# One program order for TensorE through the mixer, and the output projection in two parts instead of three

## The chip, the cores and the metric

The kernel runs on one core of a Trainium2 chip. The metric is the device time of one execution in microseconds: the median of three runs before the change is 1916.03 us (1914.43 to 1919.23). Line numbers are those of the kernel before, except where a line is said to be of the kernel after.

## What is computed

One layer of a hybrid decoder, with 256 positions of width 2048 in float32: a feed-forward half step, a mixer of differential attention (8 heads) beside RWKV-7 (16 heads of size 64), and a second feed-forward half step, each with a residual and a LayerNorm. The parts that matter here, cut from the reference:

```python
#  x <- LN1(alpha*x + 0.5*SwiGLU_1(x))
#  x <- LN2(alpha*x + W_out [DiffAttn(x) || RWKV7(x)])
#  x <- LN3(alpha*x + 0.5*SwiGLU_2(x))
...
# RWKV-7, per position t and head, after the token shift pr + mu * (prev - pr):
def step(state, xs):
    r_t, w_t, k_t, v_t, kk_t, a_t = xs
    sa = einsum('bhvk,bhk->bhv', state, -kk_t)
    state = state * w_t + sa * (kk_t * a_t) + v_t * k_t
    return state, einsum('bhvk,bhk->bhv', state, r_t)
...
# attention: two score maps for each head, p = softmax(s1) - lam * softmax(s2), then p @ v
```

One input projection, of 2048 rows, makes the columns of both mixers: q, k and v of attention, r, k and v of RWKV and 288 low-rank columns. The output projection, 2048 by 2048, joins them.

## The kernel before

**The weight stream.** Each large product is a stream of weight steps. A step loads two slices of 128 rows by up to 512 columns; ScalarE casts them to `wh` (L143) and VectorE takes the rest `wl` (L146). TensorE then makes six matmuls of 128x512 for one of the two tiles of 128 positions, hi by hi, hi by lo and lo by hi (L153 to L155), and six for the other tile of a step that lies two steps back in the mixer (`LAG`). A step in full flow is thus twelve large matmuls, called big matmuls below. When an accumulator is complete, its callback runs (`done(tt, acc)`).

**Blocks of the mixer.** The input projection is done block by block: the low-rank columns, then k, r, v of RWKV group 0 (8 heads), k and q of attention group 0, k and r of RWKV group 1, v of attention 0, v of RWKV 1, and k, q, v of attention 1 (L1098 to L1107). A callback copies its accumulator to SBUF (`tm`, L580), transposes it in four pieces (L584), and copies the result to `praw` (L608, L609 for the low-rank columns, L665 for r, k, v). After the second tile, `shift` makes the mix with the position before in one cycle for each of four pieces: ScalarE scales to `df` (L590), VectorE adds (L596). There is one `df` buffer.

**Background generators.** All other work of the mixer is written as Python generators that are advanced between weight steps by `run_bg`. `rwkv_group` makes the decay products and sigmoids (L731, L735), the scan (L739), the norm of k (scaling L745, square L746, product with a block of ones L753), the exponentials and products L760 to L779, the scores (`L789`, from AR and BK, masked to Q in L792), an inverse of 32 by 32 triangles on VectorE (`U`, `Y`, L828 to L839, here called the solve), transposes of BK (L811), and the recurrence over four chunks (L885 to L933): a product (L890), one with the inverse (L898), the state's addition and scaling (L906 to L916), the outputs (L923, L929). Then come the group norm (L945, L955) and the gate (L976, L979). `rwkv_values` transposes v (L701) and makes the bonus term (L713). `attn_heads` does the scores (L1027), softmax, transposes (L1050), product with v (L1059 to L1061), and norm.

**What sets the order.** In the input projection each generator has a credit (`BG` 1.6 for RWKV, `AT` 0.5 for attention) that a step adds to and each piece of work draws on; the instructions are then placed on each engine by the scheduler of the compiler's tile layer, which may put a group ahead of or behind where the program has it. In the first two of three parts of the output projection, `even` lets each generator do one piece for each step, and TensorE's order is fixed by hand there (`manual_schedule`, L1164). VectorE, ScalarE, GpSimd and the queues are always placed by the scheduler.

**The output projection.** Its 2048 rows are four quarters: attention 0, attention 1, RWKV 0, RWKV 1. `parts` (L1125) takes them as quarters 0 and 2, then 1, then 3. For each part and each of four column blocks, `o_done` (L1134) adds the accumulator to `y`; in the last part it does the LayerNorm statistics and the tail. A part of two quarters has eight slices of 128 rows, four pairs, so 24 matmuls for an accumulator and tile; a part of one has half of that. `ready(q)` (L1114) drains the generators of a quarter and splits its result into `xh` and `xl` (L89, L90).

Of the kernel before, what the change touches and what calls it, by code (L numbers as in the profile page):

```python
# [16 lines left out]
P = 128  # L17
# [18 lines left out]
BG = 1.6  # L36
AT = 0.5


def build(tc, A, out):  # L40
# [58 lines left out]
    class Stream:  # L99
        def __init__(self):  # L100
            self.pend = []
            self.tail = []
            self.roles = None
            self.behind = []
            self.acc = {}
            self.bg = []
            self.credit = {}
            self.hooks = {}
            self.step = 0
            self.slot = 0  # L110
            self.even = False
            self.hold = {}

# [157 lines left out]
        def flush(self, lag=0):  # L271
# [9 lines left out]
            while self.pend:  # L281
                self.mm(self.pend.pop(0), 1)

        def spawn(self, gen, rate):
            self.bg.append(gen)
            self.credit[gen] = [0.0, rate]

        def run_bg(self):
            if self.even:
                for g in list(self.bg):  # L290
                    if self.hold.get(g):
                        self.hold[g] -= 1
                        continue
                    while g in self.bg:
                        try:
                            if next(g) != 0:
                                break
                        except StopIteration:
                            self.bg.remove(g)
                return  # L300
            for g in list(self.bg):
                c = self.credit[g]
                c[0] = min(c[0], 0.0) + c[1]
                while c[0] > 0 and g in self.bg:
                    try:
                        cost = next(g)
                    except StopIteration:
                        self.bg.remove(g)
                        break
                    if cost is None:  # L310
                        break
                    c[0] -= cost
# [246 lines left out]
    def mix(mp, pq, C):  # L559
# [17 lines left out]
        def chan_major(acc, tt, widths, dst):  # L577
# [3 lines left out]
            tr = bank("tr", (P, 4, P))  # L581
            o = 0
            for i, w in enumerate(widths):
                T.transpose(tr[:w, i, :], tm[:, o:o + w], ident)  # L584
                o += w
            dst(tr)
# [12 lines left out]
        def lora_done(tt, acc):  # L599
            if tt == 0:  # L600
                pr = hp.tile([P, 4, S + 1], F32, tag="J1", name=nm("praw"))
                V.memset(pr[:, :, 0:1], 0.0)
                lora["raw"] = pr
            pr = lora["raw"]

            def dst(tr):
                c = slice(1 + tt * P, 1 + (tt + 1) * P)
# [3 lines left out]
            chan_major(acc, tt, [P, P, 32], dst)  # L611
            if tt == 1:
# [12 lines left out]
                lora.update(tw=tw, g1=g1, g2=g2)  # L625

# [20 lines left out]
        def rwkv_start(g, prev=None):  # L647
# [5 lines left out]
            stream.spawn(st["gen"], BG)  # L653
            return st

        def rwkv_cols(g, st, parts):
            gr = st["group"]

            def done(tt, acc, i):
                if tt == 0:  # L660
                    pr = hp.tile([P, 4, S + 1], F32, tag="J1" if g == 0 and i == 2 else "H3", name=nm("praw"))
                    V.memset(pr[:, :, 0:1], 0.0)
                    st["raw"] = pr
                pr = st["raw"]
                chan_major(acc, tt, [P] * 4, lambda tr: SC.copy(out=pr[:, :, 1 + tt * P:1 + (tt + 1) * P], in_=tr))  # L665
                if tt == 1:
# [4 lines left out]
                    if i == 2:  # L671
                        st["gen2"] = rwkv_values(g, st)
                        stream.spawn(st["gen2"], BG)
# [17 lines left out]
        def rwkv_values(g, st):  # L691
            prev = st["prev"]
            while "rk" not in st or (prev is not None and "chain" not in prev):
                yield None
            vp, vv, rk = st["group"].vp, st["group"].vv, st["rk"]
            SV = hp.tile([P, 4, 4, 2, 64], F32, tag="J1", name=nm("SV"))
            st["SV"] = SV
            for p in range(4):
                ps = bank("pr", (P, 4, P))
# [4 lines left out]
                yield 0.3  # L704
# [3 lines left out]
            SC.copy(out=SV[0:64, :, 3, 1, :], in_=ps[0:64, :, 64:128])  # L708
            yield 0.3
            for hf in range(2):  # L710
                ps = bank("pr", (P, 2, S))
# [3 lines left out]
                yield 0.6  # L715
            st["values"] = True

        def rwkv_group(g, st):
# [7 lines left out]
            for hf in range(2):  # L726
                for k in range(2):
                    ps = bank("pr", (P, 2, S))
                    for i in range(2):
                        c0 = (2 * hf + i) * P  # L730
                        T.matmul(ps[:, i, :], wa[:, c0:c0 + P], lora["tw"][:, k, :], start=True, stop=True)  # L731
                    for i in range(2):
                        p = 2 * hf + i
                        o, x = (tl[:, p, :], ps[:, i, :]) if k == 0 else (av[:, p], ps[:, i, :].rearrange("p (c t) -> p c t", c=4))
                        SC.activation(out=o, in_=x, func=AF.Sigmoid, bias=col(k, g, p))  # L735
                    yield 0.6
# [13 lines left out]
            for hf in range(2):  # L750
                ps = bank("pr", (P, 2, S))
# [3 lines left out]
                yield 0.6  # L755
# [38 lines left out]
            rk = t4("lw")  # L794
            for p in range(4):
                V.scalar_tensor_tensor(out=v4(rk)[:, p], in0=rh[:, p], scalar=col(4, g, p), in1=ka[:, p], op0=ALU.mult, op1=ALU.mult)
            st["rk"] = rk
            yield 1.5

            def transposed():  # L800
# [5 lines left out]
                for h in range(2):  # L806
                    for e in range(2):
                        r = slice(64 * e, 64 * e + 64)
                        ps = bank("sm", (P, 8, 64))
                        for i in range(8):  # L810
                            T.transpose(ps[:, i, :], BK[r, 2 * h + i // 4, i % 4, e:e + 2].rearrange("p a t -> p (a t)"), ident[r, r])  # L811
                        for p in range(2):
                            SC.copy(out=bt[2 * h + p][:, :, e, :], in_=ps[:, 4 * p:4 * p + 4])
# [28 lines left out]
            while "values" not in st or (g == 1 and "over" not in lora):  # L842
                st["wait"] = True
                yield None
            SV = st["SV"]
# [9 lines left out]
            if g == 1:  # L855
                yield from transposed()
# [19 lines left out]
            yield 0.6  # L876
            if g == 0:
                yield from transposed()
            BT = st["bt"]
            st["cols"] = True  # L880
# [4 lines left out]
            for c in range(4):  # L885
# [6 lines left out]
                V.tensor_copy(out=Rs, in_=ps)  # L892
                yield 0.6
# [6 lines left out]
                SC.copy(out=SV[64:128, :, c, 1, :], in_=ps[64:128])  # L900
                yield 0.6
                if c < 3:
# [14 lines left out]
                    yield 0.6 * (1 - g)  # L917
# [23 lines left out]
            for hf in range(2):  # L941
# [5 lines left out]
                yield 0.6 * (1 - g * (1 - hf))  # L947
# [3 lines left out]
            for hf in range(2):  # L951
# [5 lines left out]
                yield 0.6 * (1 - g * (1 - hf))  # L957
            SC.activation(out=merge(nrm), in_=merge(nrm), func=AF.Exp, scale=-0.5)
            yield 0.6 * (1 - g)
            V.tensor_tensor(out=merge(Yc), in0=merge(Yc), in1=merge(nrm), op=ALU.mult)  # L960
            yield 0.6 * (1 - g)
            for p in range(4):
                V.tensor_scalar(out=Yc[:, p], in0=Yc[:, p], scalar1=col(5, g, p), scalar2=col(6, g, p), op0=ALU.mult, op1=ALU.add)
            yield 0.6 * (1 - g)
            V.tensor_tensor(out=sq, in0=Yc, in1=v4(vv), op=ALU.add)
            yield 0.6 * (1 - g)
            st["gate"] = True
            while g == 0 and "v" not in st.get("next", ()):
                yield None
# [278 lines left out]
```

## Time and profile before

| what | value |
|---|---|
| median of 3 runs | 1916.03 us (1914.43 to 1919.23) |
| profiled execution, its own time | 1915.6 us |
| span of the profiled execution | 1913.8 us |
| granted TensorE clock, mean | 0.995 |
| first feed-forward, to its LayerNorm | about 0 to 716 us |
| input projection of the mixer | about 716 to 1076 us |
| output projection | about 1076 to 1197 us |
| second LayerNorm and second feed-forward | 1197 to 1913.8 us |

Rows of the trace's timeline have the start in us, the duration in us, the engine (PE is TensorE, PEld its weight loads, DVE VectorE, ACT ScalarE), the line, the operation, output and inputs, the shapes, and the number of instructions joined in the row; square brackets give the idle time ahead and what ended it. Rows of the waits give what waited, for what, the sum in us, how many times, and the longest. Rows of groups give, after the bar, the busy time in us and the mean of one instruction in ns. A matmul of 128x512 shows a duration of about 0.39 us, but starts follow each other in 0.23, since they are pipelined.

### The profile page before, as it was taken

The page shows a single profiled execution, that of the slowest core. Times are in us where ns is not written, and L with a number is a line of the kernel's source. Part 1 is how long each engine was busy: PE and PEld are TensorE (multiplying, and loading weights), DVE is VectorE, ACT ScalarE, POOL GpSimd, SP SyncE. Part 2 cuts the span into 40 slices and gives each one's busy share as a digit, 9 for nine tenths or more (in the row PEclk, how much of TensorE's full clock was granted, in tenths as well). Part 3 has the DMA queues.
Part 4 walks back from the last instruction along what each step waited for, and adds up shares of the span by engine and source line. Part 5 has one row for each costly group of instructions (what it writes and reads, how often), then busy time and mean ns, then how long its engine had stood idle before and what let it go on. Part 6 is the DMA issues. An engine that isn't in the chain of part 4 may idle for free.

```text
span 1913.8 us, 24938 instructions
## 1 busy us (share of the span) xinstructions
PE 1883.6 (98%) x9335; PEld 1549.8 (81%) x9335; DVE 1624.6 (85%) x1834; ACT 1095.3 (57%) x1376; POOL 72.6 (4%) x110
## 2 busy tenths in 40 slices
PE   9999999999999999999999999999999999999997
PEld 7888888888888888887778778788888888888886
DVE  8999987789999976777678777999999778999996
ACT  6656665556666536656555544566666545666651
POOL 0000101100000000000000000000000110000000
PEclk9999999999999999999999999999999999999999
DMA  9766676766667456555445545776666676666743
GB/s 312 247 198 218 186 239 217 233 212 199 217 216 233 142 173 198 163 160 154 146 117 159 162 148 194 260 246 198 199 211 227 213 236 213 197 210 213 228 153 131
DMA packets 207320, 381.72 MB, mean 199 GB/s; under 512 B 23530, under 2 KB 25648, under 8 KB 206944
## 3 DMA queue, kind: packets, MB, share of 16 engines
q1 hardware_dynamic: 182928, 350.53, 56.5%
q0 software_dynamic: 6832, 15.32, 2.9%
q10 hardware_dynamic: 17440, 14.29, 2.6%
q8 instruction: 73, 1.20, 0.3%
q14 instruction: 47, 0.39, 0.1%
HBM read 368.29 MB, written 11.80 MB: 199 GB/s over the span
## 4 chain that ended last, share of the span: by engine, by line
PE 59%; DVE 2%; issue 1%; ACT 1%; DMA 0%; ACTq 0%; DVEq 0%
PE acc L153 18%; PE acc L154 18%; PE acc L155 18%; PE sm L789 1%; DVE wl L146 1%; PE tr L584 0%; PE tr L443 0%; PE at L1027 0%; DVE y L345 0%; PE pr L731 0%; DVE y L353 0%; PE sm L890 0%; PE sm L898 0%; DMA dY<-Y 0%; PE sm L923 0%
## 5 line engine op out<-in xcount | busy, mean ns | idle before, releaser
L143 ACT CAST wh<-raw 128x1024 fp32r<-128x1024 f32 (+2 forms) x833 | 853.7, 1049 | 604.5 <-PE acc L155 377.8
L146 DVE TENSOR_TENSOR wl<-raw,wh 128x1024 fp32r<-128x1024 f32 (+2 forms) x833 | 984.5, 1215 | 207.1 <-ACT wh L143 202.7
L154 PE MATMUL acc<-wl,xh 128*128 128x512 f32 (+1 forms) x1552 | 606.2, 392 | 1.9 <-DVE wl L146 1.9
L155 PE MATMUL acc<-wh,xl 128*128 128x512 f32 (+1 forms) x1552 | 604.8, 391 | 1.0 <-DVE xl L90 1.0
L153 PE MATMUL acc<-wh,xh 128*128 128x512 f32 (+1 forms) x1552 | 600.0, 394 | 5.2 <-ACT xh L89 3.3
L153 PEld LDWEIGHTS acc<-wh,xh 128*128 128x128 f32 x1552 | 292.7, 189 | 67.2 <-ACT xh L89 4.9
L155 PEld LDWEIGHTS acc<-wh,xl 128*128 128x128 f32 x1552 | 292.9, 189 | 61.6 <-DVE xl L90 1.7
L154 PEld LDWEIGHTS acc<-wl,xh 128*128 128x128 f32 x1552 | 292.8, 189 | 61.7 <-DVE wl L146 3.5
L224 DVE TENSOR_TENSOR raw<-raw,raw 128x2048 f32<-128x2048 f32 x112 | 256.0, 2286 | 1.1 <-DMA raw<-in_ffn_w_gate_dram 0.5
L154 PE MATMUL acc<-wl,hh 128*128 128x512 f32 x544 | 212.0, 390 | 0.0
L155 PE MATMUL acc<-wh,hh 128*128 128x512 f32 x544 | 211.4, 389 | 0.0
L153 PE MATMUL acc<-wh,hh 128*128 128x512 f32 x544 | 210.9, 390 | 0.0
L153 PE MATMUL acc<-wh,s 128*128 128x512 f32 x448 | 174.9, 390 | 1.0 <-ACT acc L250 1.0
L155 PE MATMUL acc<-wh,s 128*128 128x512 f32 x448 | 174.6, 390 | 0.0
L154 PE MATMUL acc<-wl,s 128*128 128x512 f32 x448 | 174.3, 389 | 0.0
L153 PEld LDWEIGHTS acc<-wh,hh 128*128 128x128 f32 x544 | 102.1, 188 | 21.8 <-ACT wh L143 0.4
L155 PEld LDWEIGHTS acc<-wh,hh 128*128 128x128 f32 x544 | 102.1, 188 | 21.1
L154 PEld LDWEIGHTS acc<-wl,hh 128*128 128x128 f32 x544 | 102.2, 188 | 20.9
L153 PEld LDWEIGHTS acc<-wh,s 128*128 128x128 f32 x448 | 84.1, 188 | 19.1 <-ACT acc L250 1.5
L154 PEld LDWEIGHTS acc<-wl,s 128*128 128x128 f32 x448 | 84.1, 188 | 17.4
L155 PEld LDWEIGHTS acc<-wh,s 128*128 128x128 f32 x448 | 84.1, 188 | 17.4
L237 ACT COPY acc<-acc 128x512 f32<-128x512 f32 x28 | 16.0, 572 | 51.5 <-PE acc L155 47.8
(264 smaller groups left out, 1095.6 us busy)
## 6 DMA issues: line engine op xcount, KB each, us to landing
raw<-in_ffn_w_up_dram SPq DMA_DIRECT2D x176, 512.0 KB, 5.5
raw<-in_ffn_w_down_dram SPq DMA_DIRECT2D x176, 512.0 KB, 5.5
raw<-in_ffn_w_gate_dram SPq DMA_DIRECT2D x175, 512.0 KB, 4.7
raw<-in_w_in_dram SPq DMA_DIRECT2D x96, 512.0 KB, 3.6
raw<-in_w_out_dram SPq DMA_DIRECT2D x32, 512.0 KB, 4.2
sd<-s POOLq DMA_DIRECT2D x16, 256.0 KB, 4.1
s<-sd POOLq DMA_DIRECT2D x16, 256.0 KB, 5.0
xs<-y ACTq DMA_DIRECT2D x16, 256.0 KB, 2.6
```

The source lines that it names most:

```text
L143: SC.copy(out=wh[:, c, :w], in_=raw[:, c, :w])
L146: self.cut = V.tensor_tensor(out=wl[:, c, :w], in0=raw[:, c, :w], in1=wh[:, c, :w].bitcast(F32), op=ALU.subtract).ins
L153: T.matmul(a, hi, wh[:, j, :w], start=first and j == 0, stop=False, skip_group_check=True)
L154: T.matmul(a, hi, wl[:, j, :w], start=False, stop=False, skip_group_check=True)
L155: i = T.matmul(a, lo, wh[:, j, :w], start=False, stop=last and j == 1, skip_group_check=True)
L224: V.tensor_tensor(out=out, in0=x, in1=y, op=ALU.subtract)
L237: SC.copy(out=u, in_=a)
L789: T.matmul(pe[e][:, c, :], BK[r, p, c, e:e + 2].rearrange("p a t -> p (a t)"), AR[r, p, c].rearrange("p a t -> p (a t)"), start=True, stop ...
```

## The change

TensorE's order is fixed by hand from the start of the first RWKV group to the last part of the output projection (`ordered`), so on TensorE the order of the program is the order of execution there. The credits go: each generator does one piece for each weight step, everywhere. Some pieces are joined or cut anew (other `yield` values; two PSUM banks, `pr` and `sm`, for pairs of products). The transposes of a finished accumulator and what follows them are put off to the next step (`put`, `turn`, `then`). The fourth chunk's transposes of BK, which nothing reads, go. Attention does q before k, and its second group moves ahead of RWKV 1's v. The projection's parts become quarters 0 and 2, then 1 and 3. The diff's core:

```diff
-BG = 1.6
-AT = 0.5
...
         def run_bg(self):
-            if self.even:
...
+            while self.puts and self.puts[0][0] < self.step:
+                self.puts.pop(0)[1]()
             for g in list(self.bg):
-                c = self.credit[g]
-                c[0] = min(c[0], 0.0) + c[1]
-                while c[0] > 0 and g in self.bg:
+                if self.hold.get(g):
+                    self.hold[g] -= 1
+                    continue
+                while g in self.bg:
                     try:
-                        cost = next(g)
+                        if next(g) != 0:
+                            break
...
-        def chan_major(acc, tt, widths, dst):
+        def chan_major(acc, tt, widths, dst, then):
             tm = mp.tile([P, NB], F32, tag="tm", name=nm("tm"), bufs=2)
             SC.copy(out=tm[:, :tot], in_=acc[:, :tot])
-            tr = bank("tr", (P, 4, P))
...
+            def turn():
+                tr = bank("tr", (P, 4, P))
+                o = 0
+                for i, w in enumerate(widths):
+                    T.transpose(tr[:w, i, :], tm[:, o:o + w], ident)
+                    o += w
+                dst(tr)
+                if tt == 1:
+                    then()
+            stream.put(turn)
...
-                        for i in range(8):
-                            T.transpose(ps[:, i, :], BK[r, 2 * h + i // 4, i % 4, e:e + 2].rearrange("p a t -> p (a t)"), ident[r, r])
+                        for i in range(6):
+                            T.transpose(ps[:, i, :], BK[r, 2 * h + i // 3, i % 3, e:e + 2].rearrange("p a t -> p (a t)"), ident[r, r])
...
+        ordered = ExitStack()
+        ordered.enter_context(tc.manual_schedule(engines={mybir.EngineType.PE}))
         r1 = rwkv_start(0)
         rwkv_cols(0, r1, (1, 0, 2))
         r2 = rwkv_start(1, r1)
         a1 = attn_cols(0)
         rwkv_cols(1, r2, (1, 0))
         attn_values(0, a1)
+        a2 = attn_cols(1)
         rwkv_cols(1, r2, (2,))
-        stream.drain(gens(a1))
-        a2 = attn_cols(1)
         attn_values(1, a2)
...
-        parts = [(0, 2), (1,), (3,)]
+        parts = [(0, 2), (1, 3)]
...
-            stream.even = i < len(parts) - 1
-            with tc.manual_schedule(engines={mybir.EngineType.PE}) if stream.even else ExitStack():
-                part(i, qs)
+            if i == len(parts) - 1:
+                ordered.close()
+            part(i, qs)
```

How the order moves is seen at three places. The first is TensorE's order before, where the low-rank columns' second accumulator is transposed (L584, `tr` from `tm`); L731, the first reader of the result, follows 35 rows later.

```order
L153 MATMUL acc_6066<-wh_5997,xh_5770 128x512
L584 MATMUL tr_6015<-ident,tm_6013 128x128 x2
L584 MATMUL tr_6015<-ident,tm_6013 32x128
L154 MATMUL acc_6066<-wl_5998,xh_5770 128x512
L154 MATMUL acc_5980<-wl_6057,xh_5689 128x512
L155 MATMUL acc_5980<-wh_6056,xl_5690 128x512
```

The same place on TensorE after (L575 are the transposes, L735 the products with `tw`, L150 to L152 the big matmuls):

```order
L152 MATMUL acc_6029<-wh_5970,xl_5771 128x512
L575 MATMUL tr_6036<-ident,tm_6015 128x128 x2
L575 MATMUL tr_6036<-ident,tm_6015 32x128
L735 MATMUL pr_6060<-tw,cum_5967 128x256 x2
L735 MATMUL sm_6061<-tw,cum_5967 128x256 x2
L150 MATMUL acc_5974<-wh_6072,xh_5689 128x512
```

The products now stand directly behind the transposes, and the big matmuls behind the products.

The second place is the first k of RWKV on TensorE, after the change. L575 are the transposes of its second tile; L757 (L753 before) reads `tl`, the square made from the shifted k.

```order
L575 MATMUL tr_6242<-ident,tm_6221 128x128 x4
L150 MATMUL acc_6182<-wh_6271,xh_5689 128x512
...
L152 MATMUL acc_6235<-wh_6205,xl_5771 128x512
L757 MATMUL pr_6287<-tl_5966,bones 128x256 x2
L757 MATMUL sm_6291<-tl_5966,bones 128x256 x2
L150 MATMUL acc_6182<-wh_6297,xh_5699 128x512
```

Between L575 and L757 are twelve big matmuls; in the order before, 71 big matmuls lie between L584 and L753 there. The first r has the same distance of twelve after, from L575 to the scores (L793 after, L789 before).

The third place is VectorE's order after, at the third chunk of group 0's recurrence. L917 and L921 (L911 and L915 before) make the new state and its scaled copy SV, which TensorE's L890 reads; L828 to L778 belong to group 1, L143 is a cast.

```order
L917 TENSOR_TENSOR St_7783<-sm_7774,St_7664 128x256
L828 MEMSET Y_8170 64x1024
L143 TENSOR_TENSOR wl_7923<-raw_7920,wh_7922 128x1024
L773 TENSOR_TENSOR BK_6620<-BK_6620,tl_6623 64x16x64
L774 TENSOR_TENSOR BK_6620<-BK_6620,tl_6623 64x16x64
L777 COPY PC_7969<-qq 128x16
L778 TENSOR_TENSOR AR_6619<-AR_6619,qq 128x16x63
L921 TENSOR_TENSOR SV_6757<-St_7783,PC_6426 64x4x64 x2
```

And before, at the same chunk:

```order
L911 TENSOR_TENSOR St_7333<-sm_7324,St_7261 128x256
L828 MEMSET Y_8112 64x1024
L915 TENSOR_TENSOR SV_6761<-St_7333,PC_6357 64x4x64 x2
L1074 TENSOR_SCALAR vr_8238<-ss_8237 128x2
L829 MEMSET Y_8112 64x32
```

Six instructions now stand between the state and its copy, where one stood.

More of the change, by code (lines that the diff above doesn't have):

```diff
@@ L609, in dst, with then @@
                 V.tensor_copy(out=pr[0:32, 2, c], in_=tr[0:32, 2, :])
-            chan_major(acc, tt, [P, P, 32], dst)
-            if tt == 1:
+            def then():
+                pr = lora["raw"]
                 tw = mp.tile([P, 2, S], F32, tag="tw", name="tw")
@@ L625, in lora_done @@
                 lora.update(tw=tw, g1=g1, g2=g2)
+            chan_major(acc, tt, [P, P, 32], dst, then)
         stream.block(w_in, R0 + 3072, 288, KX, x_lhs, lora_done)
@@ L659, in done, with dst, then @@
             def done(tt, acc, i):
[L660 to L666, printed above, removed]
+                def dst(tr):
+                    if tt == 0:
+                        assert i < 2 or g == 0 or "chain" in st["prev"]
+                        pr = hp.tile([P, 4, S + 1], F32, tag="J1" if i == 2 else "H3", name=nm("praw"))
+                        V.memset(pr[:, :, 0:1], 0.0)
+                        st["raw"] = pr
+                    SC.copy(out=st["raw"][:, :, 1 + tt * P:1 + (tt + 1) * P], in_=tr)
+                def then():
+                    pr = st["raw"]
                     for p in range(4):
@@ L672, in done @@
                         st["gen2"] = rwkv_values(g, st)
-                        stream.spawn(st["gen2"], BG)
+                        stream.spawn(st["gen2"])
+                chan_major(acc, tt, [P] * 4, dst, then)
             for i in parts:
@@ L691, in rwkv_values @@
         def rwkv_values(g, st):
-            prev = st["prev"]
-            while "rk" not in st or (prev is not None and "chain" not in prev):
+            gr, prev = st["group"], st["prev"]
+            while "fed" not in st or (prev is not None and "chain" not in prev):
                 yield None
-            vp, vv, rk = st["group"].vp, st["group"].vv, st["rk"]
+            vp, vv = gr.vp, gr.vv
+            rk = t4("lw") if g == 0 else mp.tile([P, 4, S], F32, tag="vv", name=nm("rk"))
+            for p in range(4):
+                V.scalar_tensor_tensor(out=v4(rk)[:, p], in0=gr.rh[:, p], scalar=col(4, g, p), in1=gr.ka[:, p], op0=ALU.mult, op1=ALU.mult)
             SV = hp.tile([P, 4, 4, 2, 64], F32, tag="J1", name=nm("SV"))
@@ L793, in rwkv_group @@
                 yield 1.2
[L794 to L798, printed above, removed]
+            st["fed"] = True
             def transposed():
@@ L841, in rwkv_group @@
             nc.scalar.dma_start(out=dYT, in_=U[0:32])
-            while "values" not in st or (g == 1 and "over" not in lora):
-                st["wait"] = True
+            yield 0.6
+            while g == 0 and "values" not in st:
                 yield None
-            SV = st["SV"]
             TT = hp.tile([P, 16, 64], F32, tag=HT["lw"], name=nm("TT"))
@@ L876, in rwkv_group @@
             yield 0.6
+            bt = transposed()
             if g == 0:
-                yield from transposed()
-            BT = st["bt"]
-            st["cols"] = True
+                yield from bt
+            while "turned" not in st or (g == 1 and "over" not in lora):
+                yield None
+            SV = st["SV"]
             Yc = be
@@ L1045, in attn_heads @@
                 yield 0.6
-                while g == 1 and not stream.even:
-                    yield None
                 tr = bank("at", (P, 4, P))
@@ L1053, in attn_heads @@
                 yield 0.6
+                wait = "v" not in st
                 while "v" not in st:
                     yield None
+                if wait and heads[0] == 1:
+                    yield 0.6
                 vt = st["v"]
@@ L1103, in mix @@
         attn_values(0, a1)
+        a2 = attn_cols(1)
         rwkv_cols(1, r2, (2,))
-        stream.drain(gens(a1))
-        a2 = attn_cols(1)
         attn_values(1, a2)
         stream.flush()
-        while "wait" not in r2:
-            stream.advance(r2["gen"])
         lora["over"] = True
```

146 lines of the change are left out of this document (68 added, 78 removed).

## The prediction

> **What bounds the kernel now.** I read the page's busy shares first, then busy time by stage, then TensorE's waits in the stage that the diff touches. The first fence is the page's first part; the second gives, for each stretch, its length and then busy time and instructions of PE, PEld, DVE, ACT and POOL, granted clock, DMA share and GB/s.
>
> ```profile
> span 1913.8 us, 24938 instructions
> PE 1883.6 (98%) x9335; PEld 1549.8 (81%) x9335; DVE 1624.6 (85%) x1834; ACT 1095.3 (57%) x1376; POOL 72.6 (4%) x110
> ```
>
> ```profile
> 0.00:716.00 716.00, 707.95 (x3189) 586.68 (x3190) 632.74 (x591) 420.58 (x471) 35.35 (x60) 1.00 0.66 216
> 716.00:1197.00 481.00, 475.45 (x3022) 384.42 (x3021) 356.40 (x658) 263.41 (x453) 12.21 (x14) 1.00 0.54 160
> 1197.00:1913.80 716.80, 700.22 (x3129) 578.66 (x3127) 635.41 (x587) 411.30 (x454) 25.01 (x36) 0.99 0.64 209
> ```
>
> PE is the bound, and the mixer (716 to 1197 us, the only stage that the diff edits) leaves it 481.00 - 475.45 = 5.55 us without work. Nearly all of that is a few waits for cast weights and for the split of the projection's left operand:
>
> ```profile
> PE acc L154 <- DVE wl L146: 1.9, 2, 1.1
> PE acc L153 <- ACT wh L143: 1.9, 1, 1.9
> PE acc L153 <- ACT xh L89: 1.2, 1, 1.2
> PE acc L155 <- DVE xl L90: 0.4, 1, 0.4
> ```
>
> They sum to 5.4 us. No wait on a chain (transposes, shift, score operands) is among them: those chains lie beside other matmuls. So the change can gain at most these waits, their clock loss, and whatever PE instructions it makes fewer or cheaper; it can lose wherever a chain is put in PE's way. The profiled execution took 1915.6 us, 1.8 beyond its span, and lies 0.4 below the median of 1916.03; I sum against 1915.6. About 0.3% (5.7 us) is what a measurement of this kernel can tell from no change.
>
> **What goes.** (1) The waits above: 5.4 us. The new order has them behind weight steps of twelve matmuls, so I let all go. After the first two the clock was low:
>
> ```profile
> 1076.00:1084.00 8.00, 5.33 (x24) 3.72 (x20) 4.92 (x9) 6.07 (x15) 0.00 (x0) 0.81 0.37 100
> ```
>
> ```profile
> 1078.76 0.50 PE L153 MATMUL acc<-wh,xh 128*128 128x512 f32 x1 [1.87 <-ACT wh L143]
> 1080.07 0.50 PE L154 MATMUL acc<-wl,xh 128*128 128x512 f32 x1 [0.81 <-DVE wl L146]
> 1080.41 0.40 PE L155 MATMUL acc<-wh,xl 128*128 128x512 f32 x1
> 1080.64 0.39 PE L153 MATMUL acc<-wh,xh 128*128 128x512 f32 x1
> 1081.26 0.63 PE L155 MATMUL acc<-wh,xl 128*128 128x512 f32 x1
> 1081.68 0.63 PE L153 MATMUL acc<-wh,xh 128*128 128x512 f32 x1
> ```
>
> The granted 0.81 over 8 us is a loss of 8 x 0.19 = 1.5 us; the starts are 0.42 apart (1081.26 to 1081.68) instead of 0.23 (1080.41 to 1080.64). Together 6.9 us.
>
> (2) The score matmuls of L789. Columns: start, duration, engine, line, x count.
>
> ```profile
> 808.15 1.16 PE L789 MATMUL sm<-AR,BK 64*128 64x128 f32 x16
> 1004.41 2.05 PE L789 MATMUL sm<-AR,BK 64*128 64x128 f32 x16
> ```
>
> Sixteen take 1.16 us when the two row halves alternate, and 2.05 when one half follows the other, as the scheduler put some of them. Program order alternates them always: eight groups by 1.16 = 9.3 us, against 15.5 by the rows below (11.0 + 4.5). That is 6.2 us. L811 loses its fourth chunk, 64 to 48 transposes, 16 x 4.5/64 = 1.1 us.
>
> ```profile
> L789 PE MATMUL sm<-AR,BK 64*128 64x128 f32 x96 | 11.0, 283 | 0.0
> L789 PE MATMUL pr<-AR,BK 64*128 64x128 f32 x32 | 4.5, 281 | 0.0
> L811 PE MATMUL sm<-ident,BK 64*128 64x64 f32 x64 | 4.5, 229 | 0.0
> ```
>
> (3) Small groups that the scheduler cut in two, as here:
>
> ```profile
> 885.31 0.62 PE L153 MATMUL acc<-wh,xh 128*128 128x512 f32 x2
> 885.86 0.24 PE L862 MATMUL sm<-YT,Q 32*32 32x32 f32 x2
> 886.03 0.50 PE L154 MATMUL acc<-wl,xh 128*128 128x512 f32 x1
> 886.46 1.19 PE L862 MATMUL sm<-YT,Q 32*32 32x32 f32 x62
> ```
>
> At 0.23 a matmul, two from 885.31 and one more end at 886.00; the rest of L862 starts at 886.46. The two instructions cut off cost 0.46. I count eight such fragments in the order of before that the new order joins: 8 x 0.45 = 3.6 us. **The gain is 6.9 + 6.2 + 1.1 + 3.6 = 17.8 us.** Eight additions on DVE in the projection go too (32 to 24, 0.68 each), beside a busy PE: nothing. Transposes put off by a step cost PE nothing by themselves.
>
> **What comes.** PE's queue is now the program's: what a generator issues stands where its step is, and everything behind it waits with it. Each big matmul (0.23) queued behind is the weight stream, which ends the span. So a chain from a transpose through ACT and DVE back to PE is charged in full, less the work that stands between. Twelve big matmuls (2.7 us) is the usual distance.
>
> P1, the low-rank columns: L735 (before: L731) stands right behind the three transposes. Before, it ran 8 us after them.
>
> ```profile
> 731.32 0.42 DVE L608 COPY praw<-tr 128x256 f32<-128x256 f32 x1
> 732.30 0.51 ACT L590 ACTIVATE df<-praw,vB 128x256 f32<-128x256 f32 x1
> 733.57 0.48 DVE L596 SCALAR_TENSOR_TENSOR tw<-praw,om,df 128x256 f32<-128x256 f32 x1
> 734.50 0.40 ACT L621 ACTIVATE tw<-tw 64x256 f32<-64x256 f32 x1
> ```
>
> From 731.32 to 734.90 that chain took 3.6; its durations alone sum to 1.8, with handoffs and the second copy 2.6. I take 3.5 (2.6 to 4.5).
>
> P2, the first k: transposes, copy, four cycles of shift (one df buffer, so ACT and DVE alternate), scaling, square, then L757, with twelve big matmuls between.
>
> ```profile
> 757.99 0.59 ACT L665 COPY praw<-tr 128x512 f32<-128x512 f32 x1 [0.77 <-PE tr L584]
> 758.61 0.51 ACT L590 ACTIVATE df<-praw,vB 128x256 f32<-128x256 f32 x1
> 759.16 0.48 DVE L596 SCALAR_TENSOR_TENSOR BK<-praw,om,df 128x256 f32<-128x256 f32 x1 [0.44 <-ACT df L590]
> 759.68 0.35 DVE L745 TENSOR_SCALAR AR<-BK,vB 128x256 f32<-128x256 f32 x1
> 768.52 1.05 ACT L746 ACTIVATE tl<-AR 128x1024 f32<-128x1024 f32 x1
> ```
>
> A cycle is 759.64 - 758.61, about 1.05 to 1.13; the bare chain is 0.59 + 4 x 1.1 + 0.35 + 1.05 and some handoffs = 6.7. In before it took 769.57 - 757.99 = 11.6, since wh and wl casts (1.05 and 1.22 each) come between. With one cast each the chain is 7.9, less 2.7: wait 5.1 (3.9 to 6.3).
>
> P3, the first r: the same copy and cycles, then one product of 1.16 in place of scaling and square, twelve matmuls between: 4.7 (3.7 to 5.9).
>
> ```profile
> 803.09 1.16 DVE L779 TENSOR_TENSOR AR<-AR,cum 128x1024 f32<-128x1024 f32 x1
> ```
>
> P5 and P9, v of both groups: L705 stands in the step of its transposes; copy, one or two cycles: 2.5 and 2.4 (1.8 to 3 each). P8, the last k of attention: only a copy: 0.7 (0.5 to 1). P2', the second k: like P2, with some 5.4 us of PE between, but its ACT and DVE also serve group 0's chain: 4 (1.3 to 5.5).
>
> c2, the recurrence of group 0 at its third chunk. DVE's queue has, between the state's addition (L917) and the products that L890 waits for (L921), five long instructions of group 1 and a cast:
>
> ```profile
> L828 DVE MEMSET Y<- 64x1024 f32 x2 | 1.8, 912 | 0.3 <-DVE wl L146 0.2 <-issue 0.2
> L770 DVE TENSOR_TENSOR BK<-BK,tl 64x1024 f32<-64x1024 f32 x2 | 2.4, 1223 | 0.0
> L146 DVE TENSOR_TENSOR wl<-raw,wh 128x1024 fp32r<-128x1024 f32 x129 | 157.1, 1220 | 61.6 <-ACT wh L143 60.9
> ```
>
> The memset, a cast, two products of L770's form and one with cum, put at the 1.16 of the row above: 0.91 + 3 x 1.22 + 1.16 = 5.7 ahead of L921, against the 2.7 of twelve matmuls; and the exponentials that feed them have table loads. I take 5 (1 to 9).
>
> Y1: group 1's triangular solve now lies beside the attention. By the order its 31 rounds stand in a stretch of nine weight steps of PE.
>
> ```profile
> L834 DVE TENSOR_TENSOR itmp<-U,Y 64x31 f32<-64x31 f32 (+15 forms) x62 | 20.6, 332 | 10.1 <-DMA U<-dU 8.7
> ```
>
> One group's share of L834 is 10.3 us, and L836 writes the same size after each: 20.6. Nine casts are 11, attention and chain in the stretch some 11 more: 43 us of DVE, while PE has 9 x 2.7 and some 5 of small groups, 30. Part of the 13 is covered by casts made ahead. I take 4 (0 to 8). **Sum of waits: 3.5 + 5.1 + 4.7 + 2.5 + 2.4 + 0.7 + 4 + 5 + 4 = 31.9** (16.6 to 46.2).
>
> **Clock.** By the row of 1076, a wait of 2.7 in two pieces cost 1.5. P1, P2, P3, P2' and c2 are longer: 5 x 1.5 = 7.5 (0 to 15). The Trainium skill, "TensorE: Matmul & The Clock Gate", section "HAM oscillation — how this bites in real kernels", has only idle gaps above about 3.4 us throttle the array; that speaks for a smaller loss, from four of the waits, and the sum would then be 1.5 us lower. The row of 1076 disagrees, with two gaps of 1.87 and 0.81 and a clock of 0.81, so the row decides.
>
> **The sum:** 31.9 + 7.5 - 17.8 = +21.6, so 1915.6 + 21.6 = 1937.2: slower.
>
> **Rivals.** *Faster*: the mechanism is the tail of the second LayerNorm.
>
> ```profile
> 1197.00:1210.00 13.00, 8.99 (x32) 6.36 (x31) 12.93 (x21) 5.47 (x7) 1.01 (x1) 0.76 0.51 154
> ```
>
> There PE loses 4.0 us to DVE and 13 x 0.24 = 3.1 to the clock. With two parts each accumulator has 48 matmuls (10.9 us) instead of 24, so DVE may arrive with less queued and the 7.1 may go. With all waits at their low ends and no clock loss: 1915.6 + 16.6 - 17.8 - 7.1 = 1907.3. It decides where waits and clock come under 24.9 - 5.7 = 19.2 us. For it: a waiting PE also stops the casts, since ACT's casts stand behind PE, so chains may run bare. Against: DVE has idle time before 1197, and the tail's own chain (statistics, normalization, transposes) is untouched. *Even*: low ends, no clock loss, same tail: 1914.4. *Worse*: c2, Y1 and the clock at their high ends, 4 + 4 + 7.5 more: 1952.7. For it: the 11.6 us of L665 to L746 in before. *The order is not binding* and nothing moves: 1915.6; PE's listed order after the change speaks against it.
>
> **How the numbers follow.** Forecast 0.50 (1928 to 1946 of its own), worse 0.18, faster 0.20, even 0.10, not binding 0.02. So slower 0.68, within 0.3% 0.12, faster 0.20. The range leaves out about half of the faster and of the worst ends: 1907 to 1955.
>
> **What would show it.** Right: TensorE's waits in the mixer on L735 for tw, L757 for tl, L793 for AR, L705 for vv, L890 for SV, of the sizes above, with the clock under 1 behind them; L793 groups of sixteen at 1.16. Wrong: if these waits sum to under 17 us, if the chains lie under 6 us from transpose to reader, if the tail at the second LayerNorm has no idle PE, or if PE's busy time in the mixer falls by far more than 11 us.

## The result, and the profile after

The changed kernel takes 1971.96 us (median of 4 runs, 1969.8 to 1973.29); the kernel before took 1917.12 in the runs beside it. The ratio is 1.0286 (95% interval 1.0268 to 1.0304): slower by 2.9%, some 55 us, where 21.6 were forecast.

By stages, in the same columns as before (length, busy time of PE, PEld, DVE, ACT, POOL, granted clock, DMA share, GB/s):

```profile
span 1969.0 us, 24893 instructions
PE 1895.0 (96%) x9319; PEld 1554.9 (79%) x9319; DVE 1620.6 (82%) x1826; ACT 1094.9 (56%) x1376; POOL 73.0 (4%) x110
```

```profile
716.00:1252.00 536.00, 485.80 (x3004) 390.29 (x3003) 354.45 (x653) 264.21 (x454) 12.52 (x14) 0.95 0.48 144
1252.00:1969.00 717.00, 702.67 (x3138) 580.27 (x3136) 635.40 (x587) 410.96 (x454) 25.20 (x36) 0.99 0.63 209
```

All of it lies in the mixer: it is 536.0 us long where it was 481.0, and what follows is as long as before (717.0 beside 716.8). PE has less to do there, 3004 instructions for 3022, and is still busy for longer: the clock is 0.95. TensorE's waits in the mixer, in the columns of before (sum, times, longest), the largest ones:

```profile
PE pr L757 <- ACT tl L750: 9.9, 2, 5.3
PE pr L705 <- DVE vv L591: 9.0, 2, 6.7
PE sm L793 <- DVE AR L783: 5.7, 1, 5.7
PE sm L890 <- DVE SV L921: 5.2, 1, 5.2
PE at L1100 <- DVE ot L1096: 4.5, 2, 4.2
PE pr L735 <- ACT tw L615: 3.7, 1, 3.7
PE sm L981 <- DVE Q L796: 2.3, 1, 2.3
PE at L1039 <- ACT k L1009: 1.9, 1, 1.9
PE at L1072 <- ACT qq L1009: 1.8, 1, 1.8
PE sm L811 <- ACT BT L813: 1.3, 2, 0.6
```

With the smaller rows they sum to 49.8 us, against 5.4 before: +44.4 of the 55.0. What stands behind the longer waits runs slowly. Timeline of TensorE after, at the first k:

```profile
772.43 2.07 PE L757 MATMUL pr<-tl,bones 128*128 128x256 f32 x4 [5.33 <-ACT tl L750]
774.29 1.91 PE L757 MATMUL sm<-tl,bones 128*128 128x256 f32 x4
775.65 0.99 PE L150 MATMUL acc<-wh,xh 128*128 128x512 f32 x1
776.43 0.63 PE L151 MATMUL acc<-wl,xh 128*128 128x512 f32 x1
...
778.54 0.40 PE L150 MATMUL acc<-wh,xh 128*128 128x512 f32 x1
```

The wait is 5.33 us, but the small group and six big matmuls behind it take 6.11 us more, to 778.54, at starts 0.43 apart; from there the starts are 0.23 apart again. In the mixer are eight runs like this, with 51 slow big matmuls; above 0.23 each they cost 11.9 us, and the small groups ahead of them are slow too. If TensorE's time in the mixer is counted from each start to the next, less the idle time, the big matmuls grew from 375.0 to 382.4 us and the small groups from 100.2 to 103.3: with the 44.4 of waits, that makes up the 55.0.

### The profile page after: what moved, and what is told of

It reads as the page before. It is cut to its first block, busy times and chain, and to the rows that moved or that the text cites. A ratio compares the mean times of both kernels' runs of the same rounds, so it can differ in the third digit from the quotient of the medians.

```text
span 1969.0 us, 24893 instructions
## 1 busy us (share of the span) xinstructions
PE 1895.0 (96%) x9319; PEld 1554.9 (79%) x9319; DVE 1620.6 (82%) x1826; ACT 1094.9 (56%) x1376; POOL 73.0 (4%) x110
## 5 line engine op out<-in xcount | busy, mean ns | idle before, releaser
L143 DVE TENSOR_TENSOR wl<-raw,wh 128x1024 fp32r<-128x1024 f32 (+2 forms) x833 | 983.4, 1213 | 230.8 <-ACT wh L140 226.3
L150 PE MATMUL acc<-wh,xh 128*128 128x512 f32 (+1 forms) x1552 | 612.0, 400 | 1.8 <-ACT xh L87 1.0
L152 PE MATMUL acc<-wh,xl 128*128 128x512 f32 (+1 forms) x1552 | 607.4, 392 | 0.4 <-DVE xl L88 0.4
L150 PEld LDWEIGHTS acc<-wh,xh 128*128 128x128 f32 x1552 | 295.6, 191 | 65.6 <-issue 2.4
L152 PEld LDWEIGHTS acc<-wh,xl 128*128 128x128 f32 x1552 | 294.9, 190 | 62.3 <-DVE xl L88 1.1
L152 PE MATMUL acc<-wh,hh 128*128 128x512 f32 x544 | 211.4, 389 | 0.0
L150 PE MATMUL acc<-wh,hh 128*128 128x512 f32 x544 | 210.9, 390 | 0.0
L150 PE MATMUL acc<-wh,s 128*128 128x512 f32 x448 | 174.9, 390 | 2.1 <-ACT wh L140 1.1
L152 PE MATMUL acc<-wh,s 128*128 128x512 f32 x448 | 174.6, 390 | 0.0
L150 PEld LDWEIGHTS acc<-wh,hh 128*128 128x128 f32 x544 | 102.1, 188 | 21.7 <-ACT wh L140 0.4
L152 PEld LDWEIGHTS acc<-wh,hh 128*128 128x128 f32 x544 | 102.1, 188 | 21.1
L150 PEld LDWEIGHTS acc<-wh,s 128*128 128x128 f32 x448 | 84.1, 188 | 20.3 <-ACT wh L140 1.5
L152 PEld LDWEIGHTS acc<-wh,s 128*128 128x128 f32 x448 | 84.1, 188 | 17.5
```

The lines of the kernel that those rows point to most:

```text
L143: self.cut = V.tensor_tensor(out=wl[:, c, :w], in0=raw[:, c, :w], in1=wh[:, c, :w].bitcast(F32), op=ALU.subtract).ins
L150: T.matmul(a, hi, wh[:, j, :w], start=first and j == 0, stop=False, skip_group_check=True)
L152: i = T.matmul(a, lo, wh[:, j, :w], start=False, stop=last and j == 1, skip_group_check=True)
```

## The experiments

**Is it TensorE's order at all?** `x1_free` leaves TensorE's order to the scheduler until the projection; generators, pieces and parts stay.

```diff
-        ordered.enter_context(tc.manual_schedule(engines={mybir.EngineType.PE}))
         r1 = rwkv_start(0)
...
+        ordered.enter_context(tc.manual_schedule(engines={mybir.EngineType.PE}))
         for i, qs in enumerate(parts):
```

> TensorE's order is left to the scheduler again in the input projection; everything else is as after the change (one piece for each step, transposes put off, two parts). Theory (the fixed order puts readers too near their producers): the waits of TensorE in the mixer, 50 us after the change, fall under 15 us and the time comes to 1915 to 1930. Rival (the new sequence of work itself is late, whatever TensorE's order): waits stay above 35 us and the time above 1955.

Measured: 1930.61 us, ratio 1.0075 (1.0060 to 1.0090). The order in the input projection is thus 41 of the 55 us. No wait on a shift chain is left among the big matmuls. In all 16 us of waits are left, where under 15 were expected, nearly all in one place, after the input projection's last matmul and around the first of the output projection, 1073 to 1107 us; the largest waits there:

```profile
PE at L1060 <- DVE s L1055: 4.1, 1, 4.1
PE sm L860 <- DMA YT<-dYT: 3.3, 2, 3.0
```

The time is 0.6 us above the upper end of what the theory gave, and the rest is work that was left to the end. `x10_allfree` takes the fixed order away in the projection's first part too (the second line of the diff above isn't put in).

> The changed kernel with no fixed order on TensorE at all, the projection's first part included. Theory (the 13 us of waits at the end of the input projection, with the order free up to there, come from the boundary: all that the scheduler had left has to come before the first fixed instruction): the pile goes, waits under 10 us in all, 1910 to 1924. Rival (the work is late in itself there): the waits of the attention's and of the group's last pieces stay, 1926 to 1935.

Measured: 1939.93 us, ratio 1.0122 (1.0106 to 1.0137). Neither range: the time rose, and 17 us of waits are left in the mixer. The pile went from before the first part to before the second, where `ready` drains the generators (`xh` is the split of their result); between 1135 and 1188 us only 36 big matmuls run:

```profile
1187.54 0.79 PE L150 MATMUL acc<-wh,xh 128*128 128x512 f32 x1 [5.08 <-ACT xh L87]
```

My theory of a boundary that makes the pile fell. So with TensorE's order free throughout, the changed sequence of work still costs 23 us. My reading is that pieces that come one for each step end late, and that the scheduler does not bring them forward; no run changed the pieces with the order free.

**The parts of the projection.** `x2_three` is the changed kernel with three parts.

```diff
-        parts = [(0, 2), (1, 3)]
+        parts = [(0, 2), (1,), (3,)]
```

> The changed kernel with the output projection in three parts again (quarters 0 and 2, then 1, then 3). Theory (the parts cost and bring nothing): within 3 us of the changed kernel, 1969 to 1975. Rival (two parts brought a part of the gain or of the loss): more than 6 us away.

Measured: 1973.59 us, ratio 1.0301 (1.0286 to 1.0317), against 1.0286 for the changed kernel. With the order fixed, the parts are no cause of the loss, and brought no gain that could be measured.

**What distance does to a wait.** `x3_far_k` puts two more weight steps before L757 in group 0.

```diff
             yield 1.0
+            for i in range(2 * (1 - g)):
+                yield 0.6
             for hf in range(2):
```

> The changed kernel with two more weight steps between the first k's shift and the product of its squares (L757), in group 0 alone; what follows in that group moves with it, so the scores of its r come two steps later too. Theory (a wait is the chain's length less the work between, and each is followed by a clock loss of 1.5 to 3 us): the waits of 5.3 us on tl and 5.7 us on AR go, with 3 to 5 us of clock, so 14 to 16 us less: 1956 to 1958. Rival (the wait moves to the next reader): under 5 us less, with as much waited at L793 or L705.

Measured: 1956.08 us, ratio 1.0209 (1.0192 to 1.0227), inside the forecast, but by luck: the two waits did not go. All waits of the mixer fell by 8.2 us, to 41.6: with 5.4 us more work between, L757's (L759 there) fell from 5.33 to 2.09 and that of the scores from 5.66 to 4.84; others got shorter beside them (L705 from 6.67 to 4.32, L890 from 5.20 to 0.4). Why 5.4 us of cover removed only 3.2 is seen on ScalarE; here the changed kernel, from the second shift cycle to the square:

```profile
767.14 1.04 ACT L140 CAST wh<-raw 128x1024 fp32r<-128x1024 f32 x1
768.09 0.51 ACT L585 ACTIVATE df<-praw,vB 128x256 f32<-128x256 f32 x1
769.87 0.51 ACT L585 ACTIVATE df<-praw,vB 128x256 f32<-128x256 f32 x1 [1.28 <-DVE BK L591]
771.32 1.06 ACT L750 ACTIVATE tl<-AR 128x1024 f32<-128x1024 f32 x1 [0.94 <-DVE praw L660]
```

and `x3_far_k` at the same place:

```profile
767.51 1.06 ACT L140 CAST wh<-raw 128x1024 fp32r<-128x1024 f32 x1
768.47 0.50 ACT L585 ACTIVATE df<-praw,vB 128x256 f32<-128x256 f32 x1
770.23 1.05 ACT L140 CAST wh<-raw 128x1024 fp32r<-128x1024 f32 x1 [1.26 <-PE acc L152]
771.19 0.51 ACT L585 ACTIVATE df<-praw,vB 128x256 f32<-128x256 f32 x1
772.95 1.04 ACT L140 CAST wh<-raw 128x1024 fp32r<-128x1024 f32 x1 [1.26 <-PE acc L152]
773.90 1.05 ACT L750 ACTIVATE tl<-AR 128x1024 f32<-128x1024 f32 x1
```

Casts follow TensorE. While it stands, they stop once those under way are done, and the stretch from the cast at 767.14 to the square at 771.32 takes 4.2 us; while it works, a cast comes between each two cycles, and the same stretch takes 6.4, longer by just the missing 2.2.

**What a wait costs beside its length.** `x4_fill` and `x6_fill2` put useless matmuls into the three longest waits of group 0, and write into the bank that the waiting ones then overwrite; the numbers are those of the second.

```diff
                 ps = bank(("pr", "sm")[hf * (1 - g)], (P, 2, S))
+                for i in range(12 * (1 - g) * (1 - hf)):
+                    T.matmul(ps[:, 0, :], C["bones"], C["smask"], start=True, stop=True)
...
                 pe = [bank("sm", (P, 4, P)), bank(("sm", "pr")[p % 2], (P, 4, P))]
+                for i in range(13 * (1 - g) * (p == 0)):
+                    T.matmul(pe[0].rearrange("p a b -> p (a b)")[:, 0:256], C["bones"], C["smask"], start=True, stop=True)
...
                 ps = bank(("pr", "sm")[p % 2], (P, 4, P))
+                for i in range(15 * (1 - g) * (p == 0)):
+                    T.matmul(ps.rearrange("p a b -> p (a b)")[:, 0:256], C["bones"], C["smask"], start=True, stop=True)
```

> The changed kernel with idle time of TensorE filled by useless matmuls into the bank that the waiting ones then overwrite: 24 ahead of L757, 26 ahead of L793 and 30 ahead of L705, all in group 0, some 0.2 us each. The chains are as long as before. Theory (a wait costs its length and, behind it, matmuls at a low clock): idle time falls by some 15 us and the time by 5 to 9 us, the matmuls after the three places run at full clock. Rival (the slow matmuls behind the waits have another reason): the time stays within 3 us of 1972.

Measured: 1981.78 us, ratio 1.0342 (1.0326 to 1.0357). The test was mis-sized: a matmul of this form is two passes in the trace and takes about twice the 0.2 us that I had put, so 80 of them outlast the three waits (17.7 us in sum). It tells nothing of the clock. The second:

> As the kernel with useless matmuls ahead of L757, L793 and L705 in group 0, but with 12, 13 and 15 of them, since each takes 0.38 us and not 0.2; they then fit into the waits of 5.3, 5.7 and 6.7 us. Theory (idle time costs its length and then a low clock): the idle time at the three places falls under 3 us in sum, nothing of the chains changes, and the time falls by 6 to 9 us through the clock alone: 1963 to 1966. Rival (the slow matmuls have another reason): within 3 us of 1972.

Measured: 1966.59 us, ratio 1.0257 (1.0237 to 1.0277). TensorE's timeline at the first k, useless matmuls in L759, the real ones in L761:

```profile
765.81 5.34 PE L759 MATMUL pr<-smask,bones 128*128 128x256 f32 x23
771.09 1.16 PE L761 MATMUL pr<-tl,bones 128*128 128x256 f32 x4
...
772.78 0.60 PE L150 MATMUL acc<-wh,xh 128*128 128x512 f32 x1
773.22 0.40 PE L151 MATMUL acc<-wl,xh 128*128 128x512 f32 x1
...
774.36 0.39 PE L150 MATMUL acc<-wh,xh 128*128 128x512 f32 x1
```

The chain ends no earlier, yet the group and six big matmuls now take 771.09 to 774.36, 3.27 us in place of 6.11: the idle time, not the chain, made them slow, and this wait had a price of 2.8 us beside its 5.33. No wait over 0.2 us is left at the three places. The time fell by 5.4 us between the medians, 0.6 short of the forecast, for 17.7 us of filled waits; L1039's wait, at 1.9 in the changed kernel's trace, is 3.6 in this one.

**The wait at L705,** which was 6.67 us for a forecast of 2.5. In the trace after, ScalarE's `df` of the first cycle was ready at 840.52, but VectorE came to it at 844.86. I suspected the solve, whose first round stood 2.83 us for the transfer that brings U:

```profile
835.05 0.20 DVE L834 TENSOR_TENSOR itmp<-U,Y 64x31 f32<-64x31 f32 x1 [2.83 <-DMA U<-dU]
...
843.45 1.21 DVE L143 TENSOR_TENSOR wl<-raw,wh 128x1024 fp32r<-128x1024 f32 x1
...
844.86 0.47 DVE L591 SCALAR_TENSOR_TENSOR vv<-praw,om,df 128x256 f32<-128x256 f32 x1
```

`x5_solve` starts the solve three steps later in the program.

```diff
-            yield 0.6
+            for i in range(4):
+                yield 0.6
             for j in range(31, 0, -1):
```

> The changed kernel with the solve's first round put three weight steps later in both groups, nothing else. In the changed kernel VectorE stands 2.8 and 5.6 us idle at the solve's first instruction, for the transfer that brings U, and what is queued behind it comes late. Theory (that idle time made L705's wait 4 us longer than the shift alone, and made the 4.3 us at L1100): the wait at L705 of group 0 falls from 6.7 to 2 to 4 us, the one at L1100 from 4.3 to under 1, with some clock: 1961 to 1966. Rival (VectorE has simply too much to do there): both waits stay within 1.5 us, the time within 3 us of 1972.

Measured: 1969.43 us, ratio 1.0279 (1.0263 to 1.0294), waits of 7.2 at L705 and 6.1 at L1100 (L1101 there). But the edit did not do what it says: VectorE's order is the scheduler's, and in group 0 the first round still stands ahead of the shift. In group 1 VectorE still stands 4.73 us for U ahead of the attention's norm (5.63 in the changed kernel), and the wait at L1100 rose from 4.25; its cause was not tested by any other run. `x8_queue` adds to this kernel an edge that keeps group 0's solve behind the shift.

```diff
-            V.scalar_tensor_tensor(out=dst, in0=x1, scalar=om[:n, mi:mi + 1], in1=d, op0=ALU.mult, op1=ALU.add)
+            return V.scalar_tensor_tensor(out=dst, in0=x1, scalar=om[:n, mi:mi + 1], in1=d, op0=ALU.mult, op1=ALU.add).ins
...
-                        shift(pr, p, 8 * i + 4 * g + p, d)
+                        st["last"] = shift(pr, p, 8 * i + 4 * g + p, d)
...
+                with tc.issue_after(st["last"]) if g == 0 and j == 31 else ExitStack():
                     V.tensor_tensor(out=tv, in0=U[:, 0:j, j:j + 1].to_broadcast([64, j, 32 - j]),
```

> The changed kernel with the solve of group 0 truly behind the shift of its v on VectorE (in the kernel that only moved the solve's program place, the scheduler left it where it was: VectorE stood 3.4 us before it and the wait at L705 stayed at 7.2). Theory (what made L705's wait 4 us longer than the shift is what stands ahead of it in VectorE's queue, an idle wait for U's transfer and the first rounds of the solve): the wait at L705 falls from 6.7 to 2 to 4 us and the time by 3 to 6 us. Rival (the queue is long without the solve, or the shift itself is slow): the wait stays above 5 us.

Measured: 1970.94 us, ratio 1.0288 (1.0271 to 1.0305). VectorE and ScalarE there:

```profile
839.82 0.51 ACT L585 ACTIVATE df<-praw,vB 128x256 f32<-128x256 f32 x1
840.47 0.48 DVE L591 SCALAR_TENSOR_TENSOR vv<-praw,om,df 128x256 f32<-128x256 f32 x1
```

L705 now waits 2.49, so the other 4.2 us were the queue ahead of the shift. The forecast 3 to 6 us did not come. Against `x5_solve`, which lacks the edge alone, L705 fell by 4.7, but L735 waits 1.52 (0.33 there), the next k's transposes 1.57 (under 0.2), L1039 of group 0 1.41 (0.76), and smaller rises make up the rest. VectorE's work was moved, and the order fixed on TensorE lets it be late elsewhere.

**All distances at once.** `x7_far` has two steps more before L735 of group 0, three before both L757, two before the scores of group 0 and both L705, group 1's decay products behind group 0's recurrence, the solve three steps later, attention one step, and three pieces joined to make room.

```diff
+            for i in range(2 * (1 - g)):
+                yield 0.6
             for k in range(2):
...
+            while prev is not None and "chain" not in prev:
+                yield None
             SC.activation(out=tl, in_=cum, func=AF.Exp, scale=LDEC)
...
-                            stream.hold[x] = i
+                            stream.hold[x] = i + 1
```

> The changed kernel, TensorE's order still fixed, with the readers moved away from their producers: two steps more at the low-rank products, three at both L757, two at the scores of group 0, two at both L705, group 1's decay products behind group 0's recurrence, the solve three steps later, attention one step later; three pieces of group 0 and 1 joined to make room. Theory (the loss is distance, and what is cheaper in TensorE's work by the fixed order stays): the waits fall from 50 to under 15 us, the clock comes back, and the time is 1900 to 1915, under the kernel before. Rival (the casts that run beside the added matmuls lengthen the chains as fast as the distance grows, or the end of the recurrence is late): above 1925.

Measured: 1944.18 us, ratio 1.0144 (1.0127 to 1.0161). The waits fell to 29 us, not under 15, and came in new places, most of them behind VectorE; the largest two:

```profile
PE sm L803 <- DVE AR L791: 4.0, 1, 4.0
PE sm L803 <- DVE og L996: 3.6, 1, 3.6
```

The time is in the rival's range. Its reasons, longer chains or a late recurrence, were not told apart; what the rows show is that steps added by hand move work into each other's way.

**The order fixed only where there is room.** `x9_late` leaves the first half to the scheduler.

```diff
-        ordered.enter_context(tc.manual_schedule(engines={mybir.EngineType.PE}))
         r1 = rwkv_start(0)
...
+        ordered.enter_context(tc.manual_schedule(engines={mybir.EngineType.PE}))
         a2 = attn_cols(1)
```

> The changed kernel with TensorE's order fixed only from the second attention group's columns on; before that the scheduler places it. Theory (the waits of the first half, 38 us, come from the fixed order there; those of the second half, about 12, from the fixed order here): the first half has under 3 us of waits, the second some 12, and the time is 1915 to 1932. Rival (the scheduler leaves the generators' work late, and it piles up where the fixed order begins, as at the projection with the order free in the whole first part): above 1935 with 10 us and more of waits in one place.

Measured: 1938.64 us, ratio 1.0116 (1.0101 to 1.0131). The first half has 0.3 us of waits, as the theory said, but the rival's signs came: a time above 1935, and over 10 us of waits in one place. It is a place that I had not seen, L860 behind the solve of group 1:

```profile
PE sm L860 <- DMA YT<-dYT: 24.1, 2, 23.8
```

The solve starts at 1016.0 us, beside 1023.8 in the changed kernel, but TensorE no longer waits ahead of it and is further on: some 52 big matmuls lie between the solve's start and L860 here, and some 192 lay between them there. `x11_late_y` adds ten steps before it.

```diff
-            yield 0.6
-            yield 0.6
+            for i in range(2 + 10 * g):
+                yield 0.6
             Qf = Q.rearrange("p a c e t -> p (a c) e t")
```

> As the kernel with TensorE's order fixed only from the second attention group's columns on, and with L860 of group 1, which waited 23.8 us there for the end of the solve, ten weight steps (120 big matmuls, 27 us) later. Theory (in a fixed order a wait is the chain's length less the work that the program puts between): the 23.8 us go, under 8 us of waits are left in the mixer, and the time is 1911 to 1917, at the kernel before or just under it. Rival (the solve slows with the casts that the added matmuls bring, or the end of the recurrence is late): 8 us and more are still waited at L860 or in the projection, 1920 to 1930.

Measured: 1915.50 us, ratio 0.9996 (0.9987 to 1.0005): level with the kernel before. The wait of 23.8 us is gone, 7.3 us are left in the mixer, as forecast, and these are the largest:

```profile
PE pr L705 <- DVE vv L591: 2.6, 1, 2.6
PE sm L811 <- ACT BT L813: 1.3, 2, 0.6
PE at L1039 <- ACT k L1009: 1.1, 1, 1.1
PE at L1060 <- DVE s L1055: 1.1, 1, 1.1
```

`x12_late_all` moves L705 of group 1 and the attention's scores one step later too (of both groups; the first group's lie where the order is free).

```diff
+            for i in range(1 * g):
+                yield 0.6
             SV = hp.tile([P, 4, 4, 2, 64], F32, tag="J1", name=nm("SV"))
...
-                            stream.hold[x] = i
+                            stream.hold[x] = i + 1
```

> The same, with the second v's transposes (L705) and the second attention group's scores one weight step later too. Theory: the waits of 2.4 us at L705 and 0.8 at L1039 go as well, 1908 to 1915, faster than the kernel before by 0.1 to 0.4%. Rival: other waits take their place, and the time is within 2 us of the kernel with L860 alone moved.

Measured: 1920.38 us, ratio 1.0019 (1.0010 to 1.0028): 5 us slower than without, which is neither the theory nor the rival's 2 us. L1039 waits no more, but L705 still waits 2.8 and L860 waits 4.45 again: the solve starts 0.2 us later than without and ends 2.2 later, and the transfer that brings YT lands up to 5.1 us after its issue, where it took 2.2 to 2.3. Why is not shown. No version of these beat the kernel before.

## Why the prediction was wrong in size

**Right:** the direction and the mechanism. The readers that the prediction named are those that wait, nearly at its sizes: L735 3.68 (3.5 forecast), L757 5.33 and 4.54 (5.1 and 4), L793 5.66 (4.7), L890 5.20 (5), L705 of group 1 2.36 (2.4). At c2 the queue was as forecast: from the state's addition to its scaled copy VectorE did the memset, a cast and three long products. For Y1 the number is luck: the solve's end is not waited for, and the 4.25 us at L1100 are another wait. There VectorE had attention's norm behind the solve's first rounds, but no run took that away.

**Wrong, first: the sum of waits,** 31.9 forecast, 49.8 measured. The term P5 failed: I counted the shift's own cycles and not what stood ahead of them in VectorE's queue, 4.2 us by `x8_queue`, though I had done just that for c2. L1039 was 1.2 too small, the scores' 1.0. Some 10 us more are waits that I put at nothing, 0.3 to 2.3 each, at readers such as L981, L1072 and L811: in a fixed order every reader close to its producer is a candidate, not only the long chains.

**Wrong, second and as large: the clock.** I took 1.5 us a wait, from a place where 2.7 us of waits in two pieces came before. The length of the mixer grew by 55.0; less 44.4 of waits, 10.6 are left, and with the 12.4 us that I had put for cheaper work (17.8 less the 5.4 of waits) the clock would be 23.0, not 7.5. Of that 11.9 are counted in the slow big matmuls. The small groups behind the waits took some 8 us longer than groups of the same line and size without a wait ahead (for the first k, than in `x6_fill2`). That makes some 20 us of clock. Less the 1.5 of before and the 10.6, some 8 us are left for the cheaper work, which the prediction put at 10.9; this split is an estimate from the trace. That idle time is the reason was shown for one wait, of 5.33 us, at a cost of 2.8.

**Wrong, third: the gain at the scores.** TensorE's groups by line after (busy us, mean ns, idle before), and the first rows of one group of scores:

```profile
L793 PE MATMUL sm<-AR,BK 64*128 64x128 f32 x96 | 11.5, 323 | 6.5 <-DVE AR L783 5.7 <-DVE og L985 0.8
L793 PE MATMUL pr<-AR,BK 64*128 64x128 f32 x32 | 5.5, 321 | 0.0
L811 PE MATMUL sm<-ident,BK 64*128 64x64 f32 x48 | 3.9, 231 | 1.3 <-ACT BT L813 1.3
```

```profile
813.53 0.37 PE L793 MATMUL sm<-AR,BK 64*128 64x128 f32 x1
813.53 0.37 PE L793 MATMUL pr<-AR,BK 64*128 64x128 f32 x1
```

The rows for `sm` and `pr` must not be added, as I did for the kernel before: the two run side by side. Counted once, the scores are busy for 11.5 us, and were for 14.7 before, not 15.5. So they gained 3.2 us and not 6.2. Five of the eight groups of sixteen take the 1.16 us that I put; the other three stand behind waits and take 2.0 to 2.5, one of them with 0.85 of idle time within. So a part of the gain is bound to the absence of waits, and I had added the two as if apart. L811 gained 0.6 us (4.5 to 3.9) for 1.1. The 3.6 us for joined fragments were not measured alone.

**The rivals.** The faster one fell in both halves. The chain of the first k did run nearly bare while TensorE stood, with one cast on each engine, and its wait was still 5.3. At the tail of the second LayerNorm TensorE's waits fell from 4.0 to 2.2 us (3.8 in `x2_three`, with three parts), but the stage as a whole is no shorter.

**The range** ended at 1955. Its upper part had c2, Y1 and the clock at their high ends, but no place for waits that were not listed, and its clock loss ended at 15 us.

## What to carry to other kernels

Here, fixing TensorE's program order put the handoffs of its small work on the critical path, wherever the program had less work between than the chain takes with the casts that this work brings along. In such a stream price a wait of several us at its length and a third to a half as much again for the slow matmuls behind it (5.4 us for 17.7 filled, 2.8 for 5.33), and look at what stands ahead in each queue that the chain passes, not at the chain's own durations. An order by hand does no harm where the distances are long already: `x11_late_y`, with the order fixed in the second half alone and L860 moved, is as fast as the kernel before, and 15 us faster than `x1_free`, where the scheduler has the whole input projection.

## What the runs showed of the hardware that was not expected

A wait of 5.33 us was followed by 6.1 us of TensorE at half speed. Waits of 1.76 and 1.89 us in the changed kernel had no slow matmuls behind them, and one of 2.36 us had three slow big ones:

```profile
1116.73 1.12 PE L705 MATMUL pr<-ident,vv 128*128 128x128 f32 x4 [2.36 <-DVE vv L591]
...
1119.13 0.63 PE L151 MATMUL acc<-wl,xh 128*128 128x512 f32 x1
1119.56 0.52 PE L152 MATMUL acc<-wh,xl 128*128 128x512 f32 x1
```

In `x7_far` a wait of 2.02 us between big matmuls had eight slow ones directly behind it:

```profile
788.08 0.63 PE L151 MATMUL acc<-wl,xh 128*128 128x512 f32 x1 [2.02 <-DVE wl L143]
788.50 0.63 PE L152 MATMUL acc<-wh,xl 128*128 128x512 f32 x1
```

The Trainium skill, "TensorE: Matmul & The Clock Gate", section "HAM oscillation — how this bites in real kernels", puts the limit at idle gaps of about 3.4 us. Here gaps of 2.36 and 2.02 were enough, so the measurement decides.
